# A two-block image transformer on one core: all small tiles placed ahead of the large ones in SBUF

## The chip, the cores and the metric

The kernel runs on one core of a Trainium2 chip. The metric is the device time of one execution in microseconds, start to end; the lower the better. The time of the kernel before is the median of three runs.

## The reference

Two transformer blocks over 256 latent tokens and 256 context tokens of width 1024, all in float32. Block 0 mixes by retention (4 heads, key width 256, value width 512, forward and backward decay), block 1 by neighbourhood attention (32 heads of width 32). Each block is followed by a squared-ReLU MLP of hidden width 4096. Shift, scale and gate come from a conditioning vector through one large product.

```python
mod = (silu_c @ ada_w[i] + ada_b[i])[:, None, :]          # shift, scale, gate, twice
h = x * (1.0 + sc1) + sh1
y, yc = retention_mixer(...)       # block 0;  neighbourhood_mixer(...) in block 1
x = layer_norm(DN_ALPHA * x + g1 * y, ln_g[i, 0], ln_b[i, 0])
h = x * (1.0 + sc2) + sh2
x = layer_norm(DN_ALPHA * x + g2 * (square(relu(h @ w1)) @ w2), ln_g[i, 1], ln_b[i, 1])
# the context stream goes through block 0 in the same way; only x is returned
```

## The kernel before

Every large product is done in three matmuls. A float32 operand is split into a high part (rounded to the type `fp32r`) and a low part (what the rounding lost), and `mm3` (L175) issues high times high, high times low and low times high into the same PSUM bank. In matmul rows of the profile the names after the arrow are the operands, sorted by name: `pq<-hTh,lo` reads activations `hTh` and a weight part `lo`. One operand of each matmul is loaded into the array first (LDWEIGHTS, 128x128), the other streams past it (the moving operand, 256 or 512 columns).

Weights flow in a fixed list of 512 KB units. `fetch` (L250) loads a unit into `raw` over SyncE's queue (4 buffers), ScalarE casts it into `hi`, and `lows` (L268) has VectorE subtract `hi` from `raw` into `lo` (5 buffers each). `take` (L273) hands the next units to the matmuls and keeps up to five units ahead. Activations of the mixers and of the first MLP product lie in `hTh` and `hTl` (high and low part, features down the partitions). Everything of a single stage, such as queries, keys, values, masked scores, the MLP's hidden activations and attention's probabilities, lies in nine shared areas (`arena`, slots by tag, 8 KB each per partition). `scp` holds eight 2 KB scratch tiles.

TensorE takes the stages in this order: block 0 head by head (`pq` queries and keys, `pv` values, `pS` scores, `pg` gates, `po` mixing, `pw` output projection), its MLP (`p`, in two halves of the hidden width), block 1 (`pn`, `pnv`, `pqk`, `ppt`, `pav`, `pnw`), its MLP (`p1t`, `p`). In all products with `hTh`/`hTl` as moving operand a weight part is the loaded one, and the other way round where a weight part moves. `po` and `pS` read arena tiles alone. At stage boundaries the order on some engines is pinned to the program's order; elsewhere the framework's scheduler orders each engine's instructions.

Addresses: a tile pool takes its place in SBUF in the order in which pools are opened (L137 to L145), and inside a pool each tag takes its place when a tile of that tag is first asked for. Every buffer is a run of bytes at the same place in each partition, rounded up to a multiple of 32 bytes; `small` (L147) rounds up to 64. So the code alone gives the distances. In bytes per partition, with pool `cpool` starting at 0:

| area | start before | modulo 512 |
|---|---|---|
| residual stream `RR` (R0, R1) | 2,496 | 448 |
| activations `hTh`, `hTl` | 19,584 and 35,968 | 128 |
| gate `G` | 52,480 | 256 |
| weights `raw`, `hi`, `lo` | 60,672 onwards, 4,096 each | 256 |
| `smp`, the small working tiles | 118,016, 4,672 long | 256 |
| scratch `scp`, shared areas `arena` | 122,688 onwards | 320 |

Before the change, weight parts thus start 128 bytes (modulo 512) after the activations, and arena and scratch 64 bytes after the weight parts. The small tiles in between make these distances: constants, LayerNorm vectors and conditioning columns ahead of `RR`; `onecol` and the four `mod` tiles (704 bytes) between `RR` and `hTh`; `lgn` and `lgm` (128 bytes) between `hTl` and `G`; `smp` (9 x 512 + 64 bytes) between `lo` and the scratch.

Of the kernel before, what the change touches and what calls it, by code (L numbers as in the profile page):

```python
# [10 lines left out]
F32 = mybir.dt.float32  # L11
# [6 lines left out]
P = 128  # L18
D = 1024
KC = D // P  # L20
# [11 lines left out]
BIG = 1.0e30  # L32

CONST_COLS = {}

LINE = 16
# [67 lines left out]
def kernel(  # L106
# [27 lines left out]
    ec = ctx.enter_context  # L134

    WB = 5
    cpool = ec(tc.tile_pool(name="cpool", bufs=1))  # L137
    rawp = ec(tc.tile_pool(name="rawp", bufs=4))
    hip = ec(tc.tile_pool(name="hip", bufs=WB))
    lop = ec(tc.tile_pool(name="lop", bufs=WB))  # L140
    smp = ec(tc.tile_pool(name="smp", bufs=4))
    scp = ec(tc.tile_pool(name="scp", bufs=8))
    arena = ec(tc.tile_pool(name="arena", bufs=1))
    dram = ec(tc.tile_pool(name="dram", bufs=1, space=DRAM))
# [2 lines left out]
    def small(pool_, n, tag, **kw):  # L147

        return pool_.tile([P, -(-n // LINE) * LINE], F32, tag=tag, **kw)[:, :n]
# [10 lines left out]
    def slot(i, shape, dt, s):  # L160

        return arena.tile(shape, dt, tag=f"s{i}", name=nm(s))
# [109 lines left out]

    def take(n, ahead=WB):  # L273
        first = taken[0]
        while len(units) < min(first + max(n, ahead), len(specs)):
            fetch(1)
            lows()
        taken[0] = first + n
        assert len(units) - len(pending) >= first + n
        return units[first : first + n]  # L280
# [34 lines left out]
    mhalf = small(cpool, 1, "mhalf", name="mhalf")  # L315
    dve.memset(mhalf[:], -0.5)

    RR = [cpool.tile([P, 2, D], F32, tag=f"R{t}", name=f"R{t}") for t in range(2)]
    R = [RR[t // 2][:, t % 2, :] for t in range(4)]

# [25 lines left out]
        sp.dma_start(out=rpb_rows[q][:, :, cs : cs + 16], in_=src)  # L346


    onecol = small(cpool, 33, "onecol", name="onecol")
    pool.memset(onecol[:], 0.0)  # L350
    pool.memset(onecol[:, 1:2], 1.0)

    mods = {}
    grow = {}
    for l in range(2):
        for w in range(2):
            mods[l, w] = cpool.tile([P, 2, KC, 2], F32, tag=f"mod{l}{w}", name=f"mod{l}{w}")
            grow[l, w] = dram.tile([2, D], F32, tag=f"grow{l}{w}", name=f"grow{l}{w}")

    def ada_load(l, k, offs):  # L360
# [316 lines left out]
    def quarter_loads(i):  # L677
        raws = ada_quarter_load(i, AQ[i % 2])
        for a, src in enumerate((x, ctx_in)):
            cols = slice(256 * i, 256 * i + 256)  # L680
            sp.dma_start(out=RR[a][:, :, cols], in_=src[0][:, cols].rearrange("(t p) c -> p t c", p=P))
        return raws
# [13 lines left out]
        return strips[t][:, 1536:2048]  # L696

    def strip_tables():
        lgn = cpool.tile([P, 2, 8], F32, tag="lgn", name="lgn")
        sp.dma_start(  # L700
            out=lgn[:, 0], in_=ret_decay[0].rearrange("(o d) h -> o (d h)", o=1).broadcast_to([P, 8])
        )
        act.activation(out=lgn[:, 0], in_=lgn[:, 0], func=AF.Exp)
        pool.tensor_scalar_mul(out=lgn[:, 0], in0=lgn[:, 0], scalar1=-1.0)
        pool.tensor_scalar_mul(out=lgn[:, 1], in0=lgn[:, 0], scalar1=256.0)
        lgm = small(cpool, 4, "lgm", name="lgm")
        pool.tensor_scalar_mul(out=lgm[:], in0=lgn[:, 0, 4:8], scalar1=-1.0)

        dt = slot(S_VL, [P, 5, 384], F32, "dt")
        sp.dma_start(out=dt[:, 0], in_=dist)  # L710
        pool.tensor_scalar_max(out=dt[:, 1], in0=dt[:, 0], scalar1=0.0)
        for i, op in ((2, ALU.min), (3, ALU.is_ge), (4, ALU.is_le)):
            pool.tensor_scalar(
                out=dt[:, i], in0=dt[:, 0], scalar1=0.0, scalar2=-1.0 if i == 2 else 1.0 / 16.0,
                op0=op, op1=ALU.mult,
            )
        return lgn, lgm, dt
# [33 lines left out]
    def quarter_weights(i):  # L751
        return take(1, 2)[0], take(1, 1 if i < 3 else WB)[0]

# [31 lines left out]
    wq, wv = quarter_weights(0)  # L785
    raws = quarter_loads(1)
    tabs = strip_tables()
    for k in range(2):
        modulate_chunk(k, chunk(k))
# [24 lines left out]
    for a in range(2):  # L814
        dve.tensor_scalar_mul(out=RR[a][:], in0=RR[a][:], scalar1=ALPHA)

# [50 lines left out]
    for h in range(RH):  # L867
# [156 lines left out]
        else:  # L1024
# [20 lines left out]
            def affine(t, pts):  # L1045
                return [mod_aff(pts[half], half, t, A, B) for half in range(2)]
# [64 lines left out]
    for hf in range(2):  # L1111
# [55 lines left out]
        for half in range(2):  # L1167
# [69 lines left out]
            f = affine(0, p)  # L1237
# [8 lines left out]
            f = affine(1, p)  # L1246
# [622 lines left out]
```

## Time and profile before

| | |
|---|---|
| median of three runs | 1251.48 us (1249.69 to 1252.56) |
| time of the profiled execution | 1249.56 us |
| its span, first to last instruction | 1247.8 us |
| TensorE matmul busy | 1214.9 us, 7069 instructions |
| VectorE, ScalarE, GpSimd busy | 809.0, 478.6, 170.8 us |
| HBM read | 188.53 MB, 156 GB/s over the span |

Times are microseconds, means of single instructions nanoseconds. All instructions of the kernel's body stand under line L85, that of the wrapper which issues them, so groups are told apart by tile names. A matmul's own duration overlaps that of the next one, since matmuls are pipelined: what one matmul costs in a stream is the distance from its start to the next start, or the length of a stretch divided by the matmuls in it.

### The profile page before, as it was taken

To read this page: it belongs to the slowest core of one execution; us is meant where nothing else is said; L and a number is where in the kernel's file an instruction comes from. 1 tells how busy PE (TensorE), PEld (TensorE's weight loads), DVE (VectorE), ACT (ScalarE), POOL (GpSimd) and SP (SyncE) were. 2 spreads that over 40 slices of the span, in tenths; PEclk is the share of its full clock that TensorE was granted. 3 is DMA by queue.
4 is the path that set the end of the run, shared out by engine and by line. 5 is a ranking of instruction groups with operands and counts; after the bars stand their busy time and mean duration, and the time that the engine had idled before them with its cause. 6 is when DMAs were issued, how large, how long until landed. Compare 5 with 4: busy or idle time off the path is not lost.

```text
span 1247.8 us, 17933 instructions
## 1 busy us (share of the span) xinstructions
PE 1214.9 (97%) x7069; PEld 998.2 (80%) x7069; DVE 809.0 (65%) x1256; ACT 478.6 (38%) x796; POOL 170.8 (14%) x202
## 2 busy tenths in 40 slices
PE   6999999999999999999999999999999989999996
PEld 4777788787877888888778778789887767999885
DVE  2598857777585477658666564467565678776445
ACT  2462121323223146441213332146465565655331
POOL 2004401420340140000110000131111110000002
PEclk9999999999999999999999999999999999999998
DMA  9666433375543224326656546326355543565650
GB/s 312 211 210 196 143 123 106 118 242 122 146 145 109 64 68 151 107 88 204 189 155 221 186 159 221 123 77 188 79 145 172 169 153 100 176 214 192 227 189 34
DMA packets 140660, 194.53 MB, mean 156 GB/s; under 512 B 22456, under 2 KB 84384, under 8 KB 140576
## 3 DMA queue, kind: packets, MB, share of 16 engines
q1 hardware_dynamic: 135872, 181.39, 46.6%
q0 software_dynamic: 3264, 9.46, 3.0%
q10 hardware_dynamic: 1440, 2.55, 0.7%
q8 instruction: 55, 0.90, 0.3%
q14 instruction: 29, 0.24, 0.1%
HBM read 188.53 MB, written 5.75 MB: 156 GB/s over the span
## 4 chain that ended last, share of the span: by engine, by line
PE 91%; DVE 4%; ACT 2%; DMA 1%; issue 0%; POOL 0%; DVEq 0%; ACTq 0%; POOLq 0%
PE p L85 41%; PE pv L85 7%; PE pq L85 7%; PE pg L85 7%; PE pw L85 6%; PE pn L85 5%; PE pnv L85 4%; PE po L85 3%; PE pada L85 2%; PE ppt L85 2%; PE pS L85 1%; PE pav L85 1%; PE pqk L85 1%; PE pnw L85 1%; DVE lo L85 1%; PE pt L85 1%
## 5 line engine op out<-in xcount | busy, mean ns | idle before, releaser
L85 DVE TENSOR_TENSOR lo<-raw,hi 128x1024 fp32r<-128x1024 f32 (+1 forms) x227 | 277.3, 1231 | 172.0 <-ACT hi L85 167.3
L85 ACT CAST hi<-raw 128x1024 fp32r<-128x1024 f32 (+1 forms) x227 | 233.6, 1038 | 364.7 <-PE p L85 192.4
L85 PE MATMUL p<-hi,hid 128*128 128x512 f32 (+1 forms) x832 | 245.5, 378 | 0.0
L85 PEld LDWEIGHTS p<-hi,hid 128*128 128x128 f32 x832 | 151.5, 188 | 32.8 <-issue 1.2
L85 PE MATMUL p<-hTh,lo 128*128 128x256 f32 (+1 forms) x512 | 169.5, 331 | 0.8 <-DVE lo L85 0.8
L85 PE MATMUL p<-hTh,hi 128*128 128x256 f32 (+1 forms) x512 | 169.9, 332 | 0.0
L85 PE MATMUL p<-hTl,hi 128*128 128x256 f32 (+1 forms) x512 | 169.5, 331 | 0.0
L85 PE MATMUL p<-lo,hid 128*128 128x512 f32 (+1 forms) x416 | 156.8, 377 | 0.0
L85 POOL TENSOR_TENSOR R<-R,acc 128x512 f32<-128x512 f32 x40 | 65.9, 1656 | 303.6 <-DVE acc L85 303.5
L85 PEld LDWEIGHTS p<-hTh,lo 128*128 128x128 f32 x512 | 96.4, 188 | 10.8 <-DVE lo L85 1.0
L85 PEld LDWEIGHTS p<-hTh,hi 128*128 128x128 f32 x512 | 96.3, 188 | 10.5 <-issue 0.8
L85 PEld LDWEIGHTS p<-hTl,hi 128*128 128x128 f32 x512 | 96.4, 188 | 10.2 <-DVE hTl L85 0.4
L85 DVE SCALAR_TENSOR_TENSOR acc<-rawa,scol,acc 128x1024 f32<-128x1024 f32 x49 | 62.2, 1282 | 44.5 <-DMA rawa<-in_ada_w_dram 44.4
L85 PEld LDWEIGHTS p<-lo,hid 128*128 128x128 f32 x416 | 78.1, 188 | 15.7
L85 DVE SCALAR_TENSOR_TENSOR strips<-rawa,scol,strips 128x512 f32<-128x512 f32 x84 | 70.1, 886 | 2.9 <-DMA rawa<-in_ada_w_dram 2.9
L85 ACT CAST hid<-r 128x256 fp32r<-128x256 f32 (+1 forms) x64 | 32.0, 501 | 80.4 <-DVE r L85 80.4
L85 POOL TENSOR_SCALAR rstd<-mv 128x1 f32<-128x1 f32 x28 | 9.8, 350 | 368.6 <-DVE mv L85 368.6
L85 ACT ACTIVATE s<-s,mn 128x512 f32<-128x512 f32 x64 | 45.5, 712 | 32.3 <-DVE mn L85 32.3
L85 DVE TENSOR_TENSOR hid<-r,hid 128x256 fp32r<-128x256 f32 (+1 forms) x64 | 34.6, 541 | 29.7 <-ACT hid L85 29.5
L85 PE MATMUL pq<-hTh,hi 128*128 128x512 f32 x128 | 51.1, 402 | 1.8 <-ACT hTh L85 1.8
L85 PE MATMUL pw<-hi,oh 128*128 128x512 f32 x128 | 51.8, 405 | 0.0
L85 PE MATMUL pg<-hi,hTh 128*128 128x512 f32 x128 | 51.5, 402 | 0.0
(192 smaller groups left out, 2260.8 us busy)
## 6 DMA issues: line engine op xcount, KB each, us to landing
raw<-in_mlp_w_dram SPq DMA_DIRECT2D x128, 512.0 KB
rawa<-in_ada_w_dram SPq DMA_DIRECT2D x80, 512.0 KB
raw<-in_ret_w_in_dram SPq DMA_DIRECT2D x46, 512.0 KB
raw<-in_nat_w_in_dram SPq DMA_DIRECT2D x24, 512.0 KB
rawq<-in_ada_w_dram SPq DMA_DIRECT2D x16, 512.0 KB
raw<-in_ret_w_o_dram SPq DMA_DIRECT2D x16, 512.0 KB
bias<-rpb_rows POOLq DMA_DIRECT2D x16, 256.0 KB, 4.2
raw<-in_nat_w_o_dram SPq DMA_DIRECT2D x8, 512.0 KB
```

The lines of the kernel that those rows point to most:

```text
L85: r = f(*args, **kwargs)
```

## The change

The pool of small working tiles is opened first, and the seven small tiles that were asked for late (`onecol`, `lgn`, `lgm`, four `mod` tiles) are asked for ahead of `RR`. No instruction is added, removed or changed, and no tile changes size.

```diff
     WB = 5
+    smp = ec(tc.tile_pool(name="smp", bufs=4))
     cpool = ec(tc.tile_pool(name="cpool", bufs=1))
     rawp = ec(tc.tile_pool(name="rawp", bufs=4))
     hip = ec(tc.tile_pool(name="hip", bufs=WB))
     lop = ec(tc.tile_pool(name="lop", bufs=WB))
-    smp = ec(tc.tile_pool(name="smp", bufs=4))
     scp = ec(tc.tile_pool(name="scp", bufs=8))
...
+    onecol = small(cpool, 33, "onecol", name="onecol")
+    lgn = cpool.tile([P, 2, 8], F32, tag="lgn", name="lgn")
+    lgm = small(cpool, 4, "lgm", name="lgm")
+    mods = {}
+    for l in range(2):
+        for w in range(2):
+            mods[l, w] = cpool.tile([P, 2, KC, 2], F32, tag=f"mod{l}{w}", name=f"mod{l}{w}")
...
     RR = [cpool.tile([P, 2, D], F32, tag=f"R{t}", name=f"R{t}") for t in range(2)]
...
-    onecol = small(cpool, 33, "onecol", name="onecol")
-    mods = {}
-            mods[l, w] = cpool.tile([P, 2, KC, 2], F32, tag=f"mod{l}{w}", name=f"mod{l}{w}")
-        lgn = cpool.tile([P, 2, 8], F32, tag="lgn", name="lgn")
-        lgm = small(cpool, 4, "lgm", name="lgm")
```

After it, 8,000 bytes of small tiles (4,672 of `smp`, 3,328 of `cpool`) stand in front, and `RR`, `hTh`, `hTl`, `G`, `raw`, `hi`, `lo`, scratch and arena follow. Each of them is a multiple of 512 bytes long, so all of them start at 320 modulo 512 on the scale of the table above. Scratch and arena keep their addresses; the other areas move.

## The prediction

> **What bounds the kernel now.** I read the page's head first, then the chain that ended last, then the waits of TensorE.
>
> ```profile
> span 1247.8 us, 17933 instructions
> PE 1214.9 (97%) x7069; PEld 998.2 (80%) x7069; DVE 809.0 (65%) x1256; ACT 478.6 (38%) x796; POOL 170.8 (14%) x202
> PE 91%; DVE 4%; ACT 2%; DMA 1%; issue 0%; POOL 0%; DVEq 0%; ACTq 0%; POOLq 0%
> ...
> PE p L85 <- DVE lo L85: 0.8, 1, 0.8
> ```
>
> TensorE is busy for 1214.9 of 1247.8 us and holds 91% of the chain. The last row is its only listed wait for a weight part in the MLPs: 0.8 us, once. So TensorE is neither waiting for weights nor for much else; only the pace of its own matmuls can move the time by per cents. A change of addresses removes no instruction. It matters if an operand's address sets that pace.
>
> So I looked for matmuls of one shape that already have different distances between their two operands, in the chain in order of time (start, length, matmuls in the piece):
>
> ```profile
> 145.32 22.40 PE pq L85 x96
> 167.72 22.40 PE pv L85 x96
> 195.92 11.14 PE pg L85 x48
> 207.06 8.20 PE po L85 x36
> 233.77 5.61 PE pw L85 x24
> 606.18 44.20 PE p L85 x189
> 1067.06 5.70 PE p L85 x48
> ```
>
> The first six are streams of 128x128 by 128x512. Per matmul: `pq` and `pv` 22.40/96 = 233.3 ns, `pg` 232.1, `pw` 233.8, `p` 233.9. `po` takes 8.20/36 = 227.8 ns. What sets `po` apart is where its operands lie: both in the arena, so loaded and moving operand start a multiple of 512 bytes apart. In `pq`, `pv`, `pg` one is a weight part and the other an activation (128 bytes apart, modulo 512); in `pw` and the 512-wide `p` one lies in the arena and the other is a weight part (64 bytes). The seventh row, 256 wide, is 118.8 ns each, at 128 bytes.
>
> The timeline of TensorE shows it matmul by matmul (start, duration). First and last row of three stretches, of one shape each:
>
> ```profile
> 184.82 0.40 PE L85 MATMUL pv<-hi,hTl 128*128 128x512 f32 x1
> ...
> 187.39 0.39 PE L85 MATMUL pv<-lo,hTh 128*128 128x512 f32 x1
> ...
> 212.16 0.39 PE L85 MATMUL po<-vh,sl 128*128 128x512 f32 x1
> ...
> 214.88 0.39 PE L85 MATMUL po<-vh,sl 128*128 128x512 f32 x1
> ...
> 404.76 0.28 PE L85 MATMUL pS<-qkh 128*128 128x256 f32 x1
> ...
> 405.48 0.40 PE L85 MATMUL pS<-qkh 128*128 128x512 f32 x1
> ```
>
> `pv` makes 11 starts in 2.57 us, 233.6 ns each. `po`, some matmuls after its beginning, makes 12 in 2.72 us: 226.7 ns. So 227.8 is the mean of an unsettled head and a settled pace of 226.7. `pS` has both operands in the arena and is 256 wide here: 6 starts in 0.72 us, 120.0 ns. That is not faster than the 118.8 of the first MLP product: equal placement helps the wide matmul and not the narrow one. One more kind of narrow matmul lies 64 bytes apart now, in the last product's split half:
>
> ```profile
> 1233.22 0.28 PE L85 MATMUL p<-lo,hid 128*128 128x256 f32 x1
> ...
> 1235.61 0.28 PE L85 MATMUL p<-lo,hid 128*128 128x256 f32 x1
> ```
>
> 21 matmuls in 2.39 us, 113.8 ns each. This kind is the fastest narrow one, and it loses its distance of 64.
>
> **The change part by part.** It adds and removes no instruction, semaphore or transfer, and moves none past another in any queue. After it activations, weight parts, arena and scratch all start at the same place modulo 512, the relation that `po` and `pS` have today.
>
> *Wide matmuls.* Their counts, from the groups kept apart by shape; the first two rows hold all of the hidden activations' matmuls, and each later row is one of `mm3`'s three equal groups:
>
> ```profile
> L85 PE MATMUL p<-hi,hid 128*128 128x512 f32 x704 | 225.9, 396 | 0.0
> L85 PE MATMUL p<-lo,hid 128*128 128x512 f32 x352 | 139.1, 395 | 0.0
> L85 PE MATMUL p<-hTh,hi 128*128 128x512 f32 x224 | 88.5, 396 | 0.0
> L85 PE MATMUL pw<-hi,oh 128*128 128x512 f32 x128 | 51.8, 405 | 0.0
> L85 PE MATMUL pg<-hi,hTh 128*128 128x512 f32 x128 | 51.5, 402 | 0.0
> L85 PE MATMUL pv<-hi,hTh 128*128 128x512 f32 x128 | 51.4, 403 | 0.0
> L85 PE MATMUL pq<-hTh,hi 128*128 128x512 f32 x128 | 51.1, 402 | 1.8 <-ACT hTh L85 1.8
> L85 PE MATMUL pnv<-hi,hTh 128*128 128x512 f32 x64 | 26.0, 406 | 0.0
> L85 PE MATMUL pn<-hTh,hi 128*128 128x512 f32 x48 | 19.5, 406 | 0.0
> L85 PE MATMUL pnw<-hi,oTh 128*128 128x512 f32 x28 | 11.6, 414 | 0.0
> ```
>
> 704 + 352 + 3 x (224 + 4 x 128 + 64 + 48 + 28) = 1056 + 3 x 876 = 3684. Each goes from 233.3 ns to a pace between 226.7 (settled) and 227.8 (as `po`, which pays for an unsettled head every 36 matmuls; the MLP's streams are longer, those of block 1 shorter). Between 3684 x 6.6 ns = 24.3 us and 3684 x 5.5 ns = 20.3 us; I take 22.0.
>
> *Narrow matmuls.*
>
> ```profile
> L85 PE MATMUL p<-hTh,hi 128*128 128x256 f32 x288 | 81.4, 283 | 0.0
> L85 PE MATMUL pn<-hTh,hi 128*128 128x256 f32 x96 | 27.4, 285 | 0.0
> L85 PE MATMUL p1t<-hi,hTh 128*128 128x256 f32 x32 | 9.2, 286 | 0.0
> L85 PE MATMUL p<-hi,hid 128*128 128x256 f32 x128 | 24.3, 277 | 0.0
> L85 PE MATMUL p<-lo,hid 128*128 128x256 f32 x64 | 17.7, 276 | 0.0
> ```
>
> The first three rows are again one group of three each: 3 x (288 + 96 + 32) = 1248 go from 118.8 to 120.0, a loss of 1.5 us. The split half's 128 + 64 = 192 go from 113.8 to 120.0, a loss of 1.2 us. The other end for both is a settled 113.8: then the 1248 gain 6.2 us and the 192 lose nothing. I take the loss, since the `pS` row is the one with the new placement; the other end is kept for the range.
>
> *Other engines.* VectorE's rate hardly knows the distance: the subtraction at equal placement (`hid`) takes 691 ns, the one 192 bytes off (`hTl`) 682 ns.
>
> ```profile
> L85 DVE TENSOR_TENSOR hid<-r,hid 128x512 fp32r<-128x512 f32 x28 | 19.3, 691 | 14.5 <-ACT hid L85 14.4
> L85 DVE TENSOR_TENSOR hTl<-aff,hTh 128x512 fp32r<-128x512 f32 x24 | 15.9, 682 | 3.8 <-ACT hTh L85 3.5
> ```
>
> 9 ns on these 24 is 0.2 us, and even on a hundred operations 0.9 us, on an engine that is idle for 35% of the span: nothing, as TensorE's stream covers it; uncovered it would be that 0.9 us. `raw`, `hi` and `lo` have equal places already. Transposes and the small float32 products also change their distance; no row shows which way, and I keep 1 us on either side for them.
>
> *What reaches the end.* 22.0 - 1.5 - 1.2 = 19.3 us of TensorE time. Of its 1214.9 busy us, 91% of 1247.8 = 1135.5 us stand on the chain, 93.5%; in the rest another engine sets the time. 19.3 x 0.935 = 18.0 us. The profiled execution took 1249.56 us, so 1231.6 for it; the median of the runs lies 1.9 us higher, so 1251.5 - 18.0 = 1233.5 us. What is late next is the same TensorE stream: at a pace 3% higher it asks for weights 3% sooner. In the stretch of the last product,
>
> ```profile
> 1125.00:1230.00 105.00, 105.00 (x629) 92.64 (x628) 53.33 (x58) 42.95 (x54) 0.00 (x0) 1.00 0.54 176
> ```
>
> TensorE is full (105.00), while VectorE (53.33), ScalarE (42.95) and the DMA engines (0.54) are about half used, at full granted clock (1.00). They have room for 3%.
>
> **One rule against it.** The trace has streams of one shape at 233.3 and 226.7 ns that differ in where the operands lie. The Trainium skill, page "SBUF — State Buffer", section "Who interferes with whom", gives TensorE two independent read ports, one for the moving operand and one for LDWEIGHTS, and says that TensorE and ScalarE never wait on anyone. By that rule no placement could change a matmul's pace and the time would stay at 1251.5 us; the two rows of the chain (`pq` and `po`) speak against it, and I go by them.
>
> **The rivals.**
>
> *No change.* `po` is faster for another reason, such as fewer transfers beside it, and placement does nothing: 1251.5 us. For it:
>
> ```profile
> 145.32:167.72 22.40, 22.40 (x98) 18.02 (x97) 19.61 (x30) 6.08 (x10) 3.93 (x2) 1.00 0.50 156
> 207.06:215.26 8.20, 8.20 (x38) 6.75 (x37) 3.49 (x7) 0.60 (x1) 2.83 (x5) 1.00 0.29 99
> ```
>
> `po` does run with VectorE (3.49 of 8.20) and DMA (0.29) less busy than `pq` has them (19.61 of 22.40; 0.50). Against it: if traffic made the difference, `pv`'s starts would scatter with it, but in the rows between the two quoted ones they alternate between steps of about 0.23 and 0.24 us throughout. That the tiles don't land as the sizes say belongs here too. The Trainium skill's rule above ("SBUF — State Buffer", "Who interferes with whom") gives this same time. Chance 0.09.
>
> *The gain is eaten.* TensorE's matmuls settle as expected, but weight units or softmax steps come later than TensorE now asks, or streams are broken so often that many stay unsettled. Half of 18 us: 1242.5 us. Against it stand the single 0.8 us wait for `lo` and the half-idle engines above. Chance 0.12.
>
> *Slower.* The narrow matmuls pay their 2.7 us, and the wide ones gain nothing because what settles `po` is not the placement. All of the loss is in the MLP of block 1 and in `pn`; 1251.5 + 2.7 = 1254.2 us. It decides if the wide pace stays above 233.3 - 2.7 us/3684 = 232.6 ns. Chance 0.05.
>
> *More.* The narrow ones settle at 113.8 too, and all is on the path: 24.3 + 6.2 = 30.5 us, 1221 us. Chance 0.06.
>
> **How the numbers follow.** The forecast itself, a gain of 12 to 25 us, has the remaining 0.68. The range 1223 to 1246 holds it, most of the eaten case and a part of the one with more: about 0.8. About 0.2%, 2.5 us, is what a measurement of this kernel can tell from no change: forecast, eaten and more make faster 0.86; no change 0.09; slower 0.05.
>
> **What would show it.** Right: in the chain `pq` and `pv` at about 21.8 us for 96 in place of 22.40, a 512-wide `p` near 227 ns, narrow `p` near 120, `po` as it is, VectorE's and ScalarE's means within 2%, no new waits of TensorE for `lo`. Wrong: wide matmuls still at 233 ns (no change, or slower if narrow ones rise), or at 227 with new TensorE idle time named after DVE or DMA (eaten).

## The result

The changed kernel takes 1233.77 us (median of four runs, 1232.81 to 1236.14) against 1251.32 us before (median of four runs, with the three runs given before among them): 17.5 us less, ratio 0.9863 with a 95% interval of 0.9845 to 0.9882. The forecast was 1233.5 us. The profiled execution took 1232.81 us with a span of 1231.0.

The head of the page of the changed kernel, and its engines on the chain that ended last:

```profile
span 1231.0 us, 17933 instructions
PE 1196.5 (97%) x7069; PEld 999.1 (81%) x7069; DVE 809.1 (66%) x1256; ACT 478.7 (39%) x796; POOL 170.7 (14%) x202
PE 85%; DVE 6%; ACT 4%; DMA 2%; issue 1%; POOL 1%; DVEq 0%; SPq 0%; ACTq 0%; POOLq 0%
```

Instruction counts are the same. VectorE, ScalarE and GpSimd are busy for as long as before, within 0.1 us each. Only TensorE changed: 1196.5 us busy in place of 1214.9. Each engine has the same instructions in the same order as before. (The body's line number is L84 here, as one line went.)

The chain in order of time, changed kernel (start, length, matmuls):

```profile
143.51 21.76 PE pq L84 x96
165.27 21.76 PE pv L84 x96
192.84 10.88 PE pg L84 x48
203.72 8.16 PE po L84 x36
230.04 5.49 PE pw L84 x24
596.34 42.98 PE p L84 x189
641.57 42.99 PE p L84 x189
685.13 43.75 PE p L84 x192
1049.85 5.75 PE p L84 x48
```

`pq` and `pv` went from 233.3 to 226.7 ns per matmul, `pg` from 232.1 to 226.7, `pw` from 233.8 to 228.8, the first wide `p` from 233.9 to 227.4. `po`, which read arena tiles before and does so now, went from 227.8 to 226.7: its first ten steps, between 224 and 236 ns before, are 226 or 227 ns now, so the unsettled beginning is gone. Two of the experiments below bear on why. The narrow `p` in the last row went from 118.8 to 119.8. In the timeline the steps of `pv` no longer alternate; the 12 starts between the two rows shown take 2.72 us, 226.7 ns each:

```profile
182.11 0.39 PE L84 MATMUL pv<-hi,hTh 128*128 128x512 f32 x1
...
184.83 0.39 PE L84 MATMUL pv<-hi,hTh 128*128 128x512 f32 x1
```

The last product's narrow half, also in the timeline, makes 21 matmuls in 2.52 us from the first of these rows to the last, 120.0 ns in place of 113.8:

```profile
1216.39 0.28 PE L84 MATMUL p<-lo,hid 128*128 128x256 f32 x1
...
1218.91 0.28 PE L84 MATMUL p<-lo,hid 128*128 128x256 f32 x1
```

The waits of TensorE for weight parts are what they were:

```profile
PE p L84 <- DVE lo L84: 0.8, 1, 0.8
```

### The profile page after: what moved, and what is told of

Same layout as the page of the kernel before. It is cut to its first block, busy times and chain, and to the rows that moved or that the text cites. A ratio compares the mean times of both kernels' runs of the same rounds, so it can differ in the third digit from the quotient of the medians.

```text
span 1231.0 us, 17933 instructions
## 1 busy us (share of the span) xinstructions
PE 1196.5 (97%) x7069; PEld 999.1 (81%) x7069; DVE 809.1 (66%) x1256; ACT 478.7 (39%) x796; POOL 170.7 (14%) x202
## 3 DMA queue, kind: packets, MB, share of 16 engines
q10 hardware_dynamic: 1440, 2.55, 0.6%
## 4 chain that ended last, share of the span: by engine, by line
PE 85%; DVE 6%; ACT 4%; DMA 2%; issue 1%; POOL 1%; DVEq 0%; SPq 0%; ACTq 0%; POOLq 0%
PE p L84 41%; PE pv L84 7%; PE pq L84 7%; PE pw L84 6%; PE pg L84 6%; PE pn L84 4%; PE pnv L84 3%; PE pada L84 2%; PE po L84 2%; ACT s L84 2%; DVE lo L84 1%; DMA rawa<-in_ada_w_dram 1%; PE ppt L84 1%; PE pS L84 1%; ACT hi L84 1%
## 5 line engine op out<-in xcount | busy, mean ns | idle before, releaser
L84 DVE TENSOR_TENSOR lo<-raw,hi 128x1024 fp32r<-128x1024 f32 (+1 forms) x227 | 278.1, 1234 | 159.4 <-ACT hi L84 158.2
L84 ACT CAST hi<-raw 128x1024 fp32r<-128x1024 f32 (+1 forms) x227 | 233.8, 1039 | 354.6 <-PE p L84 185.5
L84 PE MATMUL p<-hi,hid 128*128 128x512 f32 (+1 forms) x832 | 242.6, 374 | 0.0
L84 PEld LDWEIGHTS p<-hi,hid 128*128 128x128 f32 x832 | 152.3, 188 | 28.7 <-issue 1.2
L84 PE MATMUL p<-hTh,lo 128*128 128x256 f32 (+1 forms) x512 | 169.8, 332 | 0.8 <-DVE lo L84 0.8
L84 PE MATMUL p<-hTh,hi 128*128 128x256 f32 (+1 forms) x512 | 170.1, 333 | 0.0
L84 PE MATMUL p<-hTl,hi 128*128 128x256 f32 (+1 forms) x512 | 169.5, 331 | 0.0
L84 PE MATMUL p<-lo,hid 128*128 128x512 f32 (+1 forms) x416 | 155.5, 374 | 0.0
L84 POOL TENSOR_TENSOR R<-R,acc 128x512 f32<-128x512 f32 x40 | 65.9, 1656 | 299.0 <-DVE acc L84 298.8
L84 PEld LDWEIGHTS p<-hTh,lo 128*128 128x128 f32 x512 | 98.1, 192 | 9.8 <-DVE lo L84 1.0
L84 PEld LDWEIGHTS p<-hTh,hi 128*128 128x128 f32 x512 | 98.1, 192 | 9.5 <-issue 0.8
L84 PEld LDWEIGHTS p<-hTl,hi 128*128 128x128 f32 x512 | 98.1, 192 | 8.7
L84 DVE SCALAR_TENSOR_TENSOR acc<-rawa,scol,acc 128x1024 f32<-128x1024 f32 x49 | 62.1, 1282 | 46.7 <-DMA rawa<-in_ada_w_dram 46.6
L84 PEld LDWEIGHTS p<-lo,hid 128*128 128x128 f32 x416 | 78.4, 189 | 13.5
L84 DVE SCALAR_TENSOR_TENSOR strips<-rawa,scol,strips 128x512 f32<-128x512 f32 x84 | 69.9, 885 | 4.9 <-DMA rawa<-in_ada_w_dram 4.9
L84 ACT CAST hid<-r 128x256 fp32r<-128x256 f32 (+1 forms) x64 | 32.0, 500 | 83.5 <-DVE r L84 83.5
L84 POOL TENSOR_SCALAR rstd<-mv 128x1 f32<-128x1 f32 x28 | 9.8, 350 | 364.7 <-DVE mv L84 364.7
L84 ACT ACTIVATE s<-s,mn 128x512 f32<-128x512 f32 x64 | 45.5, 712 | 32.3 <-DVE mn L84 32.3
L84 DVE TENSOR_TENSOR hid<-r,hid 128x256 fp32r<-128x256 f32 (+1 forms) x64 | 34.6, 541 | 29.8 <-ACT hid L84 29.6
L84 PE MATMUL pq<-hTh,hi 128*128 128x512 f32 x128 | 49.9, 393 | 2.0 <-ACT hTh L84 2.0
L84 PE MATMUL pw<-hi,oh 128*128 128x512 f32 x128 | 51.3, 401 | 0.0
L84 PE MATMUL pg<-hi,hTh 128*128 128x512 f32 x128 | 51.0, 398 | 0.0
```

The source lines that it names most:

```text
L84: r = f(*args, **kwargs)
```

## The experiments

The theory: in a stream of matmuls, the distance between the start of the loaded operand and the start of the moving operand in SBUF sets the pace. Its rivals: the place of one operand by itself, the place of the small tiles or of the residual stream, and traffic of other engines beside a stream. The places that the expectations name are 128 larger, modulo 512, than on the scale of the table of addresses; distances are the same on both scales.

**All areas moved together.** `lgn` and `lgm` go to a pool behind the arena; every large area starts 128 bytes earlier.

```diff
     arena = ec(tc.tile_pool(name="arena", bufs=1))
+    tailp = ec(tc.tile_pool(name="tailp", bufs=1))
...
-    lgn = cpool.tile([P, 2, 8], F32, tag="lgn", name="lgn")
-    lgm = small(cpool, 4, "lgm", name="lgm")
+    lgn = tailp.tile([P, 2, 8], F32, tag="lgn", name="lgn")
+    lgm = small(tailp, 4, "lgm", name="lgm")
```

> The changed kernel with lgn and lgm (128 bytes) put behind the arena, so that every large area starts 128 bytes earlier and all of them still start at one place modulo 512. If the distance between the loaded and the moving operand sets the pace (my theory): as the changed kernel, 1234 us within 2 us, wide matmuls at 227 ns, narrow ones at 120. If it is the place itself (for instance all areas 448 past a multiple of 512 in the changed kernel, 320 here): the pace changes, and up to 18 us of the gain are lost.

Measured: 1234.59 us, ratio to the kernel before 0.9869 (0.9854 to 0.9884). On its chain `pq` and `pv` take 21.76 us for 96, `pg` 10.88 for 48, the same as in the changed kernel:

```profile
144.62 21.76 PE pq L84 x96
166.38 21.76 PE pv L84 x96
193.92 10.88 PE pg L84 x48
```

With all areas 128 bytes earlier the pace is the same, so the place itself does not count here.

**Activations 128 bytes off again.** `lgn` and `lgm` are asked for late, as before the change; all else stays changed.

```diff
-    lgn = cpool.tile([P, 2, 8], F32, tag="lgn", name="lgn")
-    lgm = small(cpool, 4, "lgm", name="lgm")
...
     def strip_tables():
+        lgn = cpool.tile([P, 2, 8], F32, tag="lgn", name="lgn")
+        lgm = small(cpool, 4, "lgm", name="lgm")
```

> The changed kernel with lgn and lgm asked for late again, between hTl and G: activations are 128 bytes off the weight parts again, weights, arena and scratch stay together. Distance theory: pq, pv, pg, pn, pnv and the first MLP products (2160 wide matmuls) go back to 233 ns and their 1248 narrow ones to 118.8, pw, pnw and the second MLP products stay at 227: 2160 x 5.7 ns - 1.4 us = 10.9 us, times 0.93 on the path, 1244 us. If one area's place or the small tiles' own place makes the gain: 1234 or 1251 us.

Measured: 1244.59 us, ratio 0.9945 (0.9929 to 0.9962). Its chain:

```profile
145.53 22.39 PE pq L84 x96
167.92 22.40 PE pv L84 x96
196.13 11.15 PE pg L84 x48
207.29 8.17 PE po L84 x36
233.91 5.47 PE pw L84 x24
604.10 42.98 PE p L84 x189
649.31 44.02 PE p L84 x189
1063.02 5.70 PE p L84 x48
```

The streams that read `hTh` and `hTl` are back at 233.3 ns (`pq`, `pv`), and the narrow `p` is back at 118.8. `pw` keeps its fast pace. The two pieces of 189 part company: the first is the second MLP product, which reads the arena (227.4 ns each), the second one the first product, which reads `hTh` (232.9).

**Arena and scratch 64 bytes off again.** The pool of small working tiles is opened between `lo` and the scratch, as before; all else stays changed.

```diff
-    smp = ec(tc.tile_pool(name="smp", bufs=4))
     cpool = ec(tc.tile_pool(name="cpool", bufs=1))
     rawp = ec(tc.tile_pool(name="rawp", bufs=4))
     hip = ec(tc.tile_pool(name="hip", bufs=WB))
     lop = ec(tc.tile_pool(name="lop", bufs=WB))
+    smp = ec(tc.tile_pool(name="smp", bufs=4))
```

> The changed kernel with the pool of small working tiles opened again between lo and the scratch: arena and scratch are 64 bytes off the weight parts, activations and weight parts stay together. Distance theory: pw, pnw and the second MLP products (1524 wide matmuls) go back to 233 ns, and the last product's 192 narrow ones to 113.8, the others stay at 227: 1524 x 5.8 ns - 1.2 us = 7.6 us, times 0.93, 1241 us. If the small working tiles' own place matters: 1251 us or 1234 us.

Measured: 1240.71 us, ratio 0.9917 (0.9902 to 0.9932). Its chain is the mirror image:

```profile
144.17 21.77 PE pq L84 x96
165.94 21.76 PE pv L84 x96
193.50 10.89 PE pg L84 x48
204.39 8.20 PE po L84 x36
230.90 5.60 PE pw L84 x24
598.39 44.20 PE p L84 x189
644.84 42.95 PE p L84 x189
1058.15 5.76 PE p L84 x48
```

Now `pw` and the second MLP product are slow (233.3 and 233.9 ns), and `pq`, `pv` and the first product fast. Against the kernel before on the same chip (1251.28 us), these two halves of the change gain 6.7 and 10.6 us, 17.3 together; the whole gains 16.7 in the first experiment. The halves add up, within the scatter of the runs.

`po` is a surprise in these two chains. Here it takes 8.20 us again, 227.8 ns each, although the `pg` ahead of it runs at 226.9 ns; its first ten steps are uneven in all four heads of block 0. In the experiment before it took 8.17 us, 226.9 ns each, right behind a slow `pg` (232.3), and only the first of the four heads had the uneven steps. So a slow stream ahead is not what makes them; what does is not shown.

**Equal distances without small tiles in front.** The kernel before, with `lgn` and `lgm` ahead of `RR` and the pool of small working tiles opened last.

```diff
-    smp = ec(tc.tile_pool(name="smp", bufs=4))
     scp = ec(tc.tile_pool(name="scp", bufs=8))
     arena = ec(tc.tile_pool(name="arena", bufs=1))
+    smp = ec(tc.tile_pool(name="smp", bufs=4))
...
+    lgn = cpool.tile([P, 2, 8], F32, tag="lgn", name="lgn")
+    lgm = small(cpool, 4, "lgm", name="lgm")
     RR = [cpool.tile([P, 2, D], F32, tag=f"R{t}", name=f"R{t}") for t in range(2)]
...
-        lgn = cpool.tile([P, 2, 8], F32, tag="lgn", name="lgn")
-        lgm = small(cpool, 4, "lgm", name="lgm")
```

> The kernel before with lgn and lgm asked for ahead of RR and the pool of small working tiles opened last: onecol and the mod tiles stay between RR and hTh, the small working tiles lie behind the arena, yet activations, weight parts, arena and scratch start at one place modulo 512, 384, where the weight parts lay before. RR starts elsewhere (192). Distance theory: all of the gain, 1234 us. If small tiles in front, RR's place or the weights' new place made the gain: 1251 us, or part of the gain.

Measured: 1232.67 us, ratio 0.9854 (0.9839 to 0.9868): all of the gain, with weight parts where they lay before and `RR` somewhere else. Its streams have the pace of the changed kernel:

```profile
144.11 21.76 PE pq L85 x96
595.72 42.95 PE p L85 x189
```

"In front" is not what matters. The rivals about small tiles, `RR` and the weights' own place fall.

**The pace by itself.** A kernel with nothing but matmul streams on two tiles, every distance in turn.

```diff
+    def stream(name, n, mo, wo, count=72):
+        ps = psp.tile([P, 512], F32, tag="ps", name=name)
+        for i in range(count):
+            m, w = mo // 4 + 512 * (i % 4), wo // 4 + 128 * ((5 * i) % 16)
+            pe.matmul(ps[:, :n], lhsT=W[:, w : w + 128], rhs=M[:, m : m + n], start=(i == 0), stop=(i == count - 1))
...
+    stream("wide64b", 512, 0, 64)
...
+    stream("wideboth64b", 512, 64, 64)
...
+    stream("narrow64b", 256, 0, 64)
...
```

> Leaves the whole model out: it copies x to the output and runs 26 streams of 72 matmuls each on two tiles that hold x, 13 of them 512 wide and 13 of them 256 wide. Loaded operand minus moving operand is 0, 64, 128, 192, 256, 320, 384, 448, 16 and 32 bytes modulo 512, and three streams have both operands 64, 128 and 256 bytes further on at distance 0. Distance theory: wide 226.7 ns at 0 and in the three moved ones, 233 at 64, 128 and 384 as in the kernel before; narrow 120 at 0, 113.3 at 64, 118.7 at 128 and 384. Rivals: if the place itself counts, the three moved streams differ; if traffic of other engines made the difference, all wide streams are alike, since nothing else runs here. For 192, 256, 320 and 448 and for distances under a 64-byte step I have no forecast.

Groups by line of that kernel. The number in a name is the distance in bytes, or in "both" how far both operands were moved together. The busy time is the length of a stream of 72, and less the last matmul's own duration it holds 71 steps:

```profile
L84 PE MATMUL wide64b<-mov,wts 128*128 128x512 f32 x72 | 17.0, 395 | 0.0
L84 PE MATMUL wide320b<-mov,wts 128*128 128x512 f32 x72 | 17.0, 395 | 0.0
L84 PE MATMUL wide128b<-mov,wts 128*128 128x512 f32 x72 | 16.9, 394 | 0.0
L84 PE MATMUL wide192b<-mov,wts 128*128 128x512 f32 x72 | 16.6, 391 | 0.0
L84 PE MATMUL wideboth64b<-mov,wts 128*128 128x512 f32 x72 | 16.5, 390 | 0.0
L84 PE MATMUL wide256b<-mov,wts 128*128 128x512 f32 x72 | 16.5, 389 | 0.0
L84 PE MATMUL narrow0b<-mov,wts 128*128 128x256 f32 x72 | 8.8, 283 | 0.0
L84 PE MATMUL narrow128b<-mov,wts 128*128 128x256 f32 x72 | 8.7, 281 | 0.0
L84 PE MATMUL narrow64b<-mov,wts 128*128 128x256 f32 x72 | 8.6, 281 | 0.0
```

Each of the two kernels of streams was run once. The stream at distance 0 came first and began with eight steps of 426 ns and more, so its busy time cannot be compared and is not shown. Measured from the last 48 starts of each stream in the timeline: wide 226.7 ns at 0 and 256, 233.3 at 64 and 320, 232.4 at 128 and 384, 228.9 at 192 and 448; 226.7 with both operands moved by 64, 128 or 256. So the distance counts modulo 256, not 512, and the place does not. (At 128 bytes it does not fix the pace to the last nanosecond: in the kernel before `pq` and `pv` had 233.3 ns there, with steps of 238 and 229 ns in turn, while `pg` and the first MLP product had 232.4, with the seven steps that the stream here repeats.) Below a step of 64, 16 bytes cost nothing (226.7) and 32 cost as much as 64 (233.3). No other engine had work beside these streams, and no transfer ran but the fetching of instructions (0.23 MB over the whole run), so traffic does not make the difference either. Narrow: 120.0 at 0 and 256, 117.8 at 64, 192, 320 and 448, 118.8 at 128 and 384. One number of the expectation missed: the narrow stream at 64 had 117.8, not the 113.3 of the kernel before.

**How a narrow stream is entered.** The same kernel with each narrow stream begun after 9 matmuls of another kind, or from an idle TensorE.

```diff
+    def entered(name, n, d, n0, d0):
+        run(psp.tile([P, 512], F32, tag="ps", name="lead" + name), n0, d0, 9, True)
+        run(psp.tile([P, 512], F32, tag="ps", name=name), n, d, 72, False)
...
```

> Leaves the whole model out: it copies x to the output and runs streams of 72 narrow matmuls at distances 0, 64, 128 and 192, each entered from 9 wide or 9 narrow matmuls at distance 64 or 0, and narrow and wide streams entered from an idle TensorE. If a stream at one distance has more than one settled pace and its entry chooses, narrow at 64 gives 113.3 from wide matmuls at 64 (as in the kernel before) and 117.8 from narrow ones at 0. If the distance alone sets the pace, 117.8 in all, and the 113.8 of the kernel before has to come from something else, such as its operands' order or its two moving tiles.

Groups by line of that kernel, distance first, then how it was entered:

```profile
L84 PE MATMUL n64from512at64b<-mov,wts 128*128 128x256 f32 x72 | 8.6, 281 | 0.0
L84 PE MATMUL n64from256at0b<-mov,wts 128*128 128x256 f32 x72 | 8.6, 281 | 0.0
L84 PE MATMUL n192from512at64b<-mov,wts 128*128 128x256 f32 x72 | 8.6, 280 | 0.0
L84 PE MATMUL n192from512at0b<-mov,wts 128*128 128x256 f32 x72 | 8.3, 276 | 0.0
```

At 192 the same 72 instructions settle at 117.8 or at 113.3 ns (8.6 and 8.3 us), and the entry decides. At 64 all four entries from another stream gave 117.8, but entered from an idle TensorE the stream settled at 113.3; at 192 it was 117.8 from idle. At 128 one of four entries gave 120.0 (`n128from512at0b`), the other three 118.7. And nine matmuls at 64 that followed a stream of 113.3 ns at 192 ran at 113.4 themselves (`leadn192from256at64b`). So a narrow stream has two settled paces at these distances, while the entry named in the expectation was the wrong one: what took the kernel before to 113.8 is not shown. Wide streams entered from idle had the same paces over their last 48 starts as in the first map.

**A better place for the narrow matmuls.** The latent activations of the last MLP are written 112 columns (448 bytes) or 16 columns (64 bytes) further into `hTh` and `hTl`. The loaded weights then start 64 or 192 bytes, modulo 256, after the moving activations.

```diff
     def hs(k, a, b):
+        a, b = a + off[0], b + off[0]
         return hTh[:, k, a:b], hTl[:, k, a:b]
...
-        hi, lo = hTh[:, ks, tsl(t)], hTl[:, ks, tsl(t)]
+        cols = slice(t * P + off[0], (t + 1) * P + off[0])
+        hi, lo = hTh[:, ks, cols], hTl[:, ks, cols]
...
+    off[0] = 112
```

> The changed kernel with the latent activations of the last MLP written 112 columns (448 bytes) further into hTh and hTl, so that in its first product's 672 narrow matmuls the loaded weights stand 64 bytes off the moving activations (modulo 512), as in the last product's split half before the change. If the narrow pace there is 113.8 ns as that row had it: 672 x 6.2 ns = 4.2 us less than the changed kernel, 1230 us. If it is the 117.8 ns of the stream measured alone at 64: 672 x 2.2 ns = 1.5 us less, 1232.5 us. If distance doesn't matter there: 1234 us.

> As the kernel before it, but 16 columns (64 bytes) further, which puts the loaded weights 192 bytes off modulo 256. The stream measured alone had 117.8 ns at this distance as well: 1.5 us less than the changed kernel, 1232.5 us; if only 64 has a second, faster pace, this one cannot reach 1230.

> The changed kernel itself, beside the two versions of this call on the same chip: 1234 us within 1.5 us.

Measured on one chip: 1232.61 us (1230.49 to 1233.65) and 1232.52 us (1227.99 to 1235.35), the changed kernel 1233.85 us (1233.42 to 1240.02); ratios to the kernel before 0.9851 (0.9837 to 0.9864), 0.9850 (0.9830 to 0.9871) and 0.9871 (0.9853 to 0.9890). The intervals overlap: neither is shown to be faster than the changed kernel. Their matmuls are. One stream of 48 narrow `p`, from the chain of the version at 64 and then from that at 192:

```profile
1052.08 5.66 PE p L84 x48
```

```profile
1051.21 5.45 PE p L84 x48
```

That is 117.9 and 113.5 ns, against 119.8 in the changed kernel. Over all 672 the mean step is 117.8 and 117.5 ns: at 192 the first stream settles at 113.5, the later ones nearly all at 117.8, as the map of entries has it. The expected 1.5 us is what the medians show (1.2 and 1.3), within the scatter of the runs.

## Why the prediction was right

*What bounds the kernel.* TensorE's own pace, as the prediction had it: instructions and the other engines' busy times stayed, and the span fell by nearly what the pace gave.

*Wide matmuls, 22.0 us.* Right in mechanism, 10% too large. Laying the two timelines side by side, start by start, and taking the steps that no wait breaks, the wide matmuls take 19.9 us less, 0.2 of it in `po`. Not every group ran at 233.3 ns before (by mean step, `pg`, `pnv` and the first MLP product 232.4): 0.9 ns on these 1248 matmuls is 1.1 of the 2.1 us missing. And not every group comes down to 226.7 now (by the same mean `pw` 228.2, `pnv` 228.1); that their streams are broken off more often is the likely reason, and not shown.

*Narrow matmuls, a loss of 2.7 us.* Measured 2.6: the streams that were 128 bytes off lose 1.5 and those 64 bytes off 1.1. The six `pS` starts at 120.0 ns were enough to price 1440 matmuls. The count left out 24 narrow `pnw`, which at these paces are worth under 0.2 us.

*Other engines, nothing.* VectorE's subtractions kept their 691 and 682 ns, and the latter now has equal places too, so the 9 ns between them are not the distance.

*The share on the path, 0.935.* The pace gave 17.3 us (19.9 less 2.6) and the span fell by 16.8: by this count 97% arrived. By the page's busy time, whose ends are modelled, it is 16.8 of 18.4 us, 91%. The factor lies between. It was taken from TensorE's share of the chain, and that share fell from 91% to 85% without TensorE waiting longer for weight parts (0.8 us in the MLPs both times), so it is no firm basis for such a factor. Two misses, the wide term 2.1 us too large and the factor a little low by the count of starts, offset each other in part: the forecast gain was 18.0 us, the span fell by 16.8 and the median by 17.5. That the median came within 0.3 us of the forecast is partly luck, since runs of the changed kernel spread over 3.3 us.

*The rule set against the trace.* The Trainium skill, "SBUF — State Buffer", "Who interferes with whom", has TensorE's two read ports independent and TensorE waiting on no one. That no other engine holds it up agrees with the map (233.3 ns at 64 bytes with all other engines idle). That its two reads are independent does not: the same matmuls take 226.7 or 233.3 ns when nothing but the distance of the two operands is changed. The measurement decides.

*Left open.* The runs show that the pace follows the distance, modulo 256 bytes, and for some distances also what ran before. Why it does, whether two reads meet in one part of the memory or in TensorE's own order of loads, no run here shows, and nothing was tried that would.

## What to carry to other kernels

Where TensorE bounds a kernel, measure a stream's start-to-start step by operand pair before anything else: the fastest pair in the trace shows what the others could reach, and a placement at no cost may be all that parts them. For the 128x128 by 512-column matmuls here, start loaded and moving operand a multiple of 256 bytes apart; for 256 columns a distance of 64 or 192 bytes is better per matmul (117.8 or 113.3 ns in place of 120.0), though no gain of the whole kernel was shown for it. Small tiles between large ones set these distances by accident, so put them where they can't, or check the sums of their sizes.

## What was not expected of the hardware

The distance counts modulo 256 bytes, where the change was made for 512. A stream settles into repeating steps: at 64 and 128 bytes the steps of a wide stream repeat a cycle (231 and 236 ns in turn at 64), at 0 they go to 226.7 after at most some ten matmuls. A narrow stream at 64 or 192 bytes has two such states, 113.3 and 117.8 ns, and how it is entered chooses. At 128 bytes two paces were seen as well, 118.7 and 120.0 for narrow streams and 232.4 and 233.3 for wide ones; what chooses between the wide ones was not looked into.
